# The first activation rows split straight from PSUM feature by feature, the first weight chunk split in two pieces, and the first transfers dealt out to two queues

## The chip, the cores and the metric

The kernel runs on one core of one Trainium2 chip. The metric is the device time of one execution in microseconds, as the median of several runs. TensorE (PE in the rows) does the matrix products, VectorE (DVE) and ScalarE (ACT) the element-wise work, GpSimd (POOL) a few small steps, and SyncE (SP) issues most of the transfers.

## What is computed

The reference is a decoder trunk of two layers on 256 rows of 1024 features in fp32. Each layer is

```
h = RMSNorm(x);  u = h @ w_in          # one wide input projection, columns for q, k, v, gates
o_A = sliding-window attention with sinks;  o_B = native sparse attention
x = x + RMSNorm((sigmoid(g_A) * (o_A @ W_A) + sigmoid(g_B) * (o_B @ W_B)) @ w_out)
x = x + RMSNorm(ConvGatedMLP(RMSNorm(x)))
```

The change touches only the first products of the first layer: the gain of the first RMSNorm is multiplied into `x`, the result is transposed so that features lie on the partitions, and it is multiplied with the first columns of `w_in`. The factor of the norm itself (one over the root mean square of a row) is applied later, to the products.

## The kernel before

Every fp32 operand is cut into a high and a low part (`copy` on ACT writes the high part as fp32r, `sub` on DVE writes the rest), and every product is made of three fp32r matmuls: high by high, high by low, low by high (`mm3`, L375; `products`, L438, for the first two chunks). Weights come in chunks through `Stream`: `load` (L154) issues the DMA on SP, `high` (L172) issues the ACT copy of a whole chunk and returns a function that issues the DVE subtraction. A chunk of `w_in` is 128 partitions by 2 feature blocks by 512 columns, 512 KB.

Rows are handled in two tiles `t` of 128, features in two halves `h` of four blocks of 128. The start is the function `start` (L1141). It issues some matmuls on zeros (`warm`, counts in `WARM`), transposes the gain vector to `gfirst`, and then for the first half of the features of both row tiles: `first_T` (L417) transposes four blocks of `X` into a PSUM bank of tag "T" (two buffers) and DVE multiplies the bank by the gain into an SBUF tile (L422); `first_split` (L425) copies that tile to the high part on ACT and returns the DVE subtraction for the low part. `W.high(0)` and `W.make(1)` split the first two weight chunks. The function `second` (run ahead of the first products of chunk 1) does the same for the second half of the features and for weight chunk 2. `W.make(3)` runs two steps later, and `rest` one step after that: the squares of `X` on ACT (`mean_sq`, L368), the root mean square on POOL (`rstd_of`, L362), and the rope tables (`rope_tables`, L336: a chain of DVE steps, two sines on ACT, eight multiplications on POOL).

The first tile of columns takes chunks 0 to 3 in the order of `FIRST`, row tile 0 and 1 in turn. When row tile 0 has its fourth chunk, `fin_a` (L562) makes the first rotated queries from the PSUM bank: `rope` (L486) on DVE reads the tables, ACT and DVE split the result, and `stack_T` (L497) transposes it on PE (L501). That transpose stands at a fixed place in PE's queue, between the products of the second tile of columns.

The order of the instructions in each engine's queue is not written out by hand (`MANUAL` is None). A planner sets it when the kernel is built, from the order of the text and its own idea of durations; the queue then stays as it is.

The transfers at the start: SP issues the identity and the gain, then the four chunks; ACT issues the four half-rows of `X` (L271), first half of both row tiles and then second half. A transfer takes one of eight completion semaphores in turn, so the ninth is issued when the first has landed.

Of the kernel before, what the change touches and what calls it, by code (L numbers as in the profile page):

```python
# [13 lines left out]
ALU = mybir.AluOpType  # L14
# [39 lines left out]
WARM = (6, 2, 3)  # L54
# [11 lines left out]
def tile_hybrid_trunk(  # L66
# [78 lines left out]
    class Stream:  # L145
# [26 lines left out]
        def high(self, i):  # L172
# [16 lines left out]
            copy(hi, st)  # L189

            def low():
                sub(lo, st, r32(hi))
                self.made[i] = (hi, lo, both)
                while self.front in self.made:
                    self.front += 1
# [73 lines left out]
    for h in range(2):  # L269
        for t in range(2):  # L270
            act.dma_start(halves(X[:, t, :])[h], halves(xv[:, t, :])[h])  # L271
    for i in range(4):
        W.load(i)
# [143 lines left out]
    def first_T(t, h):  # L417
        b = bank("T")
        for k in range(4):
            pe.transpose(b[:, k * P:(k + 1) * P], X[:, t, (h * 4 + k) * P:(h * 4 + k + 1) * P], ident)  # L420
        m = k2().rearrange("p (k c) -> p k c", k=4)
        dve.tensor_tensor(m, b.rearrange("p (k c) -> p k c", k=4), gfirst[:, h * 4:h * 4 + 4, None].to_broadcast([P, 4, P]), ALU.mult)  # L422
        return m

    def first_split(t, h, m, pair):  # L425
        tk = slice(t * P, (t + 1) * P)
        ho = pair[0][:, h * 4:h * 4 + 4, tk]
        copy(ho, m)
        return lambda: sub(pair[1][:, h * 4:h * 4 + 4, tk], m, r32(ho))

    def attn_layer(l, xp, rs, gains, first):
# [6 lines left out]
        def products(t, c, bk, chs, w):  # L438
            todo = [(tt, p, k) for p in ((0, 0), (0, 1), (1, 0)) for tt in range(2) for k in range(2)] if c == 0 else \
                   [(t, p, k) for p in ((0, 0), (1, 0), (0, 1)) for k in range(2)]  # L440
            if c == 0:
                todo = todo[6 * t:6 * t + 6]
            for tt, (xp_, wp_), k in todo:
# [697 lines left out]
    def start():  # L1141
# [12 lines left out]
        m0 = first_T(0, 0)  # L1154
        lw0 = W.high(0)
        low0 = first_split(0, 0, m0, xp)
        warm(WARM[1])
        low1 = first_split(1, 0, first_T(1, 0), xp)
        warm(WARM[2])
        lw0()  # L1160
        low0()
        low1()
        W.make(1)

        def second():
            m0, m1 = first_T(0, 1), first_T(1, 1)
            lw = W.high(2)
            lows = [first_split(t, 1, m, xp) for t, m in ((0, m0), (1, m1))]
            lw()
            for f in lows:  # L1170
                f()

# [96 lines left out]
```

## Time and profile before

| what | us |
|---|---|
| median of 3 runs | 783.96 (782.5 to 784.26) |
| the profiled execution, its own time | 782.81 |
| its span from the first to the last instruction | 781.0 |
| PE busy in the span | 759.2 |
| DVE busy | 613.1 |
| ACT busy | 495.4 |
| POOL busy | 34.0 |

The profiled execution is one of its own, 1.15 us below the median. Its time is 1.81 us more than its span. A busy engine in the table is one that has an instruction in flight. Matmuls overlap each other: a row of the timeline gives the start of the first of a group and the time to the end of the last, so the pace of the engine is read from starts, not from lengths. The same holds for ACT and DVE, where the next instruction starts some 0.1 us before the one before it ends.

### The profile page before, as it was taken

Reading aid. Unit: us, or ns where it says so; the run is one execution under the profiler, and the core shown is the slowest. Engines: PE = TensorE matmul, PEld = TensorE weight load, DVE = VectorE, ACT = ScalarE, POOL = GpSimd, SP = SyncE. Lnnn points to the kernel's source line nnn. Section 1 sums busy time; section 2 is a strip of 40 time slices with the busy share of each in tenths; the row PEclk is TensorE's granted clock in tenths of the full one; section 3 lists DMA queues with packets and bytes.
Section 4 is the critical chain, followed back from the end, with each engine's and each line's share of the span. In section 5 each row is a group of like instructions: output and inputs, shape, how many; then the busy total and the mean of one; then the engine's idle time right before and its main releaser. Section 6 shows DMA issues by size and latency. Waiting matters only on the chain.

```text
span 781.0 us, 12886 instructions
## 1 busy us (share of the span) xinstructions
PE 759.2 (97%) x4742; PEld 676.8 (87%) x4742; DVE 613.1 (79%) x1188; ACT 495.4 (63%) x950; POOL 34.0 (4%) x60
## 2 busy tenths in 40 slices
PE   8999999999899999999989999999999999999996
PEld 6788898887799999999868889988878999999995
DVE  6899898686787777777787989985876877677775
ACT  6596986754665555565556969866465655566552
POOL 4300001000100000000010000010010000000000
PEclk9999999999999999999999999999999999999999
DMA  8624264465566565665545323644645556656731
GB/s 337 196 86 133 64 219 170 136 188 162 173 205 189 188 187 184 209 210 188 164 134 163 95 82 121 200 153 162 200 144 172 188 187 189 188 182 201 217 104 54
DMA packets 42346, 131.26 MB, mean 168 GB/s; under 512 B 5375, under 2 KB 5931, under 8 KB 42283
## 3 DMA queue, kind: packets, MB, share of 16 engines
q1 hardware_dynamic: 41707, 129.39, 52.0%
q10 hardware_dynamic: 576, 1.05, 0.4%
q8 instruction: 37, 0.61, 0.3%
q14 instruction: 26, 0.21, 0.1%
HBM read 129.37 MB, written 1.05 MB: 167 GB/s over the span
## 4 chain that ended last, share of the span: by engine, by line
PE 83%; ACT 8%; DVE 4%; POOL 2%; issue 1%; DMA 1%; SPq 0%; DVEq 0%; POOLq 0%; ACTq 0%
PE mm L376 6%; PE mm L378 6%; PE mm L377 6%; PE T L1024 5%; PE mm L1023 5%; PE T L1023 5%; PE mm L1024 5%; PE T L1022 5%; PE mm L1022 5%; PE S L377 5%; PE S L376 5%; PE S L378 5%; PE O L376 3%; PE O L377 3%; PE O L378 3%; ACT k L635 2%
## 5 line engine op out<-in xcount | busy, mean ns | idle before, releaser
L117 DVE TENSOR_TENSOR wl<-st,wh 128x1024 fp32r<-128x1024 f32 (+2 forms) x220 | 260.4, 1186 | 101.5 <-ACT wh L114 100.3
L114 ACT ACTIVATE wh<-st 128x1024 fp32r<-128x1024 f32 (+2 forms) x220 | 225.5, 1028 | 178.1 <-PE O L378 40.5
L376 PE MATMUL mm<-wh,x 128*128 128x512 f32 (+2 forms) x248 | 92.9, 375 | 0.7 <-DVE VT L546 0.6
L377 PE MATMUL mm<-wl,x 128*128 128x512 f32 (+2 forms) x248 | 91.6, 370 | 0.0
L378 PE MATMUL mm<-wh,x 128*128 128x512 f32 (+2 forms) x248 | 91.3, 368 | 0.1
L1023 PE MATMUL mm<-q,wh 128*128 128x256 f32 x320 | 90.7, 284 | 0.0
L1024 PE MATMUL T<-q,wl 128*128 128x256 f32 x320 | 90.6, 283 | 0.0
L1023 PE MATMUL T<-q,wh 128*128 128x256 f32 x320 | 90.6, 283 | 0.0
L1024 PE MATMUL mm<-q,wl 128*128 128x256 f32 x320 | 90.6, 283 | 0.0
L1022 PE MATMUL T<-q,wh 128*128 128x256 f32 x320 | 90.5, 283 | 0.0
L1022 PE MATMUL mm<-q,wh 128*128 128x256 f32 x320 | 90.5, 283 | 0.0
L1022 PEld LDWEIGHTS mm<-q,wh 128*128 128x128 f32 x320 | 61.4, 192 | 0.9
L1022 PEld LDWEIGHTS T<-q,wh 128*128 128x128 f32 x320 | 61.4, 192 | 0.8
L1023 PEld LDWEIGHTS mm<-q,wh 128*128 128x128 f32 x320 | 61.4, 192 | 0.8
L1023 PEld LDWEIGHTS T<-q,wh 128*128 128x128 f32 x320 | 61.4, 192 | 0.7
L1024 PEld LDWEIGHTS mm<-q,wl 128*128 128x128 f32 x320 | 61.4, 192 | 0.1
L1024 PEld LDWEIGHTS T<-q,wl 128*128 128x128 f32 x320 | 61.4, 192 | 0.0
L378 PEld LDWEIGHTS mm<-wh,x 128*128 128x128 f32 x248 | 46.7, 188 | 6.1 <-DVE x L117 0.5
L376 PEld LDWEIGHTS mm<-wh,x 128*128 128x128 f32 x248 | 46.7, 188 | 6.0 <-issue 0.8
L377 PEld LDWEIGHTS mm<-wl,x 128*128 128x128 f32 x248 | 46.7, 188 | 4.8
L635 ACT ACTIVATE k<-k,mn 128x128 f32<-128x128 f32 (+1 forms) x96 | 42.4, 445 | 7.1 <-DVE mn L632 7.0
L114 ACT ACTIVATE k<-k 128x256 fp32r<-128x256 f32 x72 | 29.1, 413 | 9.1 <-DVE k L1035 5.6
(294 smaller groups left out, 1657.0 us busy)
## 6 DMA issues: line engine op xcount, KB each, us to landing
st<-in_ffn_w_up_dram SPq DMA_DIRECT2D x88, 512.0 KB, 4.2
st<-in_ffn_w_down_dram SPq DMA_DIRECT2D x44, 512.0 KB, 3.9
st<-in_w_in_dram SPq DMA_DIRECT2D x42, 512.0 KB, 3.6
st<-in_w_out_dram SPq DMA_DIRECT2D x16, 512.0 KB, 3.8
st<-in_w_in_dram SPq DMA_DIRECT2D x16, 384.0 KB, 3.1
st<-in_cmp_w_dram SPq DMA_DIRECT2D x16, 256.0 KB, 2.6
st<-in_w_branch_a_dram SPq DMA_DIRECT2D x8, 512.0 KB, 3.6
st<-in_w_branch_b_dram SPq DMA_DIRECT2D x8, 512.0 KB, 3.5
```

The source lines that it names most:

```text
L114: return act.activation(dst, src, AF.Copy, scale=scale)
L117: dve.tensor_tensor(dst, a, b, ALU.subtract)
L376: pe.matmul(o, xh, wh, start=first, stop=False, skip_group_check=True)
L377: pe.matmul(o, xh, wl, start=False, stop=False, skip_group_check=True)
L378: pe.matmul(o, xl, wh, start=False, stop=last, skip_group_check=True)
L635: last_exp[0] = act.activation(self.pt[:, hh, s, :], sm[:, :nk], AF.Exp, bias=self.mn[:, i:i + 1], scale=-1.0, accum_out=self.dn[:, i:i + 1])
L1022: pe.matmul(o, wh[:, k, :], hh[:, k, c0:c1], start=(k == 0), stop=False, skip_group_check=True)
L1023: pe.matmul(o, wh[:, k, :], hl[:, k, c0:c1], start=False, stop=False, skip_group_check=True)
L1024: pe.matmul(o, wl[:, k, :], hh[:, k, c0:c1], start=False, stop=(k == 7), skip_group_check=True)
```

## The change

`first_T` no longer multiplies by the gain: it returns the PSUM bank itself. `first_split` takes the bank and a list of feature blocks. For each block it issues one ACT copy from PSUM, 128 by 128, with the gain as the scale operand, which writes the high part; for the low part it returns a function that issues for each block one DVE `scalar_tensor_tensor` from PSUM (bank times gain minus high part). `W.high` takes a number of pieces; chunk 0 is split in two (one piece for each feature block of 128), the others in one as before. `start` orders the splits of the first half by block pairs, with the chunk copies in between, and leaves out the last three `warm` matmuls. `second` puts the splits of `X` ahead of the chunk's. `products` for chunk 0 takes the twelve matmuls in another order. The first half-row of `X` stays on ACT's queue; the other three go to SP's, between and behind the first two chunks.

```diff
-WARM = (6, 2, 3)
+WARM = (6, 2, 0)
...
-        def high(self, i):
+        def high(self, i, pieces=1):
...
-            copy(hi, st)
+            cuts = [slice(n * a // pieces, (n + 1) * a // pieces) for n in range(pieces)]
+            for c in cuts:
+                copy(hi[:, c], st[:, c])
 
             def low():
-                sub(lo, st, r32(hi))
+                for c in cuts:
+                    sub(lo[:, c], st[:, c], r32(hi[:, c]))
...
-    for h in range(2):
-        for t in range(2):
-            act.dma_start(halves(X[:, t, :])[h], halves(xv[:, t, :])[h])
-    for i in range(4):
-        W.load(i)
+    act.dma_start(halves(X[:, 0, :])[0], halves(xv[:, 0, :])[0])
+    W.load(0)
+    nc.sync.dma_start(halves(X[:, 1, :])[0], halves(xv[:, 1, :])[0])
+    W.load(1)
+    for t in range(2):
+        nc.sync.dma_start(halves(X[:, t, :])[1], halves(xv[:, t, :])[1])
+    W.load(2)
+    W.load(3)
...
-        m = k2().rearrange("p (k c) -> p k c", k=4)
-        dve.tensor_tensor(m, b.rearrange("p (k c) -> p k c", k=4), gfirst[:, h * 4:h * 4 + 4, None].to_broadcast([P, 4, P]), ALU.mult)
-        return m
-
-    def first_split(t, h, m, pair):
+        return b
+
+
+    def first_split(t, h, b, pair, ks):
         tk = slice(t * P, (t + 1) * P)
-        ho = pair[0][:, h * 4:h * 4 + 4, tk]
-        copy(ho, m)
-        return lambda: sub(pair[1][:, h * 4:h * 4 + 4, tk], m, r32(ho))
+        for k in ks:
+            act.activation(pair[0][:, 4 * h + k, tk], b[:, k * P:(k + 1) * P], AF.Copy, scale=gfirst[:, 4 * h + k:4 * h + k + 1])
+
+        def low():
+            for k in ks:
+                kk = 4 * h + k
+                dve.scalar_tensor_tensor(pair[1][:, kk, tk], b[:, k * P:(k + 1) * P], gfirst[:, kk:kk + 1], r32(pair[0][:, kk, tk]),
+                                         ALU.mult, ALU.subtract)
+        return low
...
-            todo = [(tt, p, k) for p in ((0, 0), (0, 1), (1, 0)) for tt in range(2) for k in range(2)] if c == 0 else \
-                   [(t, p, k) for p in ((0, 0), (1, 0), (0, 1)) for k in range(2)]
             if c == 0:
+                todo = [(tt, p, k) for p, tt in (((0, 0), 0), ((1, 0), 0), ((0, 0), 1), ((0, 1), 0), ((0, 1), 1), ((1, 0), 1)) for k in range(2)]
                 todo = todo[6 * t:6 * t + 6]
+            else:
+                todo = [(t, p, k) for p in ((0, 0), (1, 0), (0, 1)) for k in range(2)]
...
-        m0 = first_T(0, 0)
-        lw0 = W.high(0)
-        low0 = first_split(0, 0, m0, xp)
+        b0 = first_T(0, 0)
         warm(WARM[1])
-        low1 = first_split(1, 0, first_T(1, 0), xp)
+        b1 = first_T(1, 0)
         warm(WARM[2])
-        lw0()
-        low0()
-        low1()
-        W.make(1)
+        l00 = first_split(0, 0, b0, xp, (0, 1))
+        lw0 = W.high(0, 2)
+        l10 = first_split(1, 0, b1, xp, (0, 1))
+        l02 = first_split(0, 0, b0, xp, (2, 3))
+        l12 = first_split(1, 0, b1, xp, (2, 3))
+        lw1 = W.high(1)
+        for f in (l00, lw0, l10, l02, l12, lw1):
+            f()
 
         def second():
-            m0, m1 = first_T(0, 1), first_T(1, 1)
+            bs = [first_T(t, 1) for t in range(2)]
+            lows = [first_split(t, 1, bs[t], xp, range(4)) for t in range(2)]
             lw = W.high(2)
-            lows = [first_split(t, 1, m, xp) for t, m in ((0, m0), (1, m1))]
-            lw()
             for f in lows:
                 f()
+            lw()
```

## Rows read from the trace of the kernel before

**Rows 1.** The page: the span, the busy times of the engines, the clock granted to TensorE in 40 slices.

```profile
PE 759.2 (97%) x4742; PEld 676.8 (87%) x4742; DVE 613.1 (79%) x1188; ACT 495.4 (63%) x950; POOL 34.0 (4%) x60
...
PEclk9999999999999999999999999999999999999999
```

**Rows 2.** The chain of work that ended last, in order of time, from the start to the first transpose of rotated queries: start, length, what.

```profile
1.58 5.00 DMA st<-in_w_in_dram
...
6.60 1.06 ACT wh L114
...
12.53 1.23 ACT x L114 x2
13.76 0.52 ACT wh L114
...
20.84 3.36 POOL tab L359 x4
...
29.77 0.51 PE T L501 x4
```

**Rows 3.** The timeline of PE: start, length of the group, engine, line, operation, tiles, count, and in brackets the idle time ahead of it with what ended that.

```profile
1.44 2.92 PE L1148 MATMUL S<-k 128*128 128x512 f32 x6 [1.44 <-DVE k L1143]
4.55 0.24 PE L1152 MATMUL T<-cst,k 8*128 8x8 f32 x1 [0.19 <-DMA k<-in_attn_pre_gain_dram]
4.73 1.11 PE L420 MATMUL T<-cst,X 128*128 128x128 f32 x4
...
6.28 0.60 PE L420 MATMUL T<-cst,X 128*128 128x128 f32 x4
6.63 0.94 PE L1148 MATMUL S<-k 128*128 128x512 f32 x3
8.23 1.26 PE L445 MATMUL mm<-wh,x 128*128 128x512 f32 x4 [0.66 <-ACT x L114]
...
11.17 1.03 PE L420 MATMUL T<-cst,X 128*128 128x128 f32 x8
...
14.81 0.39 PE L376 MATMUL mm<-wh,x 128*128 128x512 f32 x1
15.04 0.39 PE L377 MATMUL mm<-wl,x 128*128 128x512 f32 x1
...
28.41 0.39 PE L376 MATMUL S<-wh,x 128*128 128x512 f32 x1
29.77 0.51 PE L501 MATMUL T<-ident_r,k 128*128 128x128 f32 x4 [0.98 <-DVE k L117]
```

**Rows 4.** The timeline of ACT, same columns.

```profile
6.60 1.06 ACT L114 ACTIVATE wh<-st 128x1024 fp32r<-128x1024 f32 x1 [2.49 <-DMA st<-in_w_in_dram]
7.56 1.13 ACT L114 ACTIVATE x<-k 128x512 fp32r<-128x512 f32 x2
...
10.40 1.06 ACT L114 ACTIVATE wh<-st 128x1024 fp32r<-128x1024 f32 x1 [0.52 <-DMA st<-in_w_in_dram]
12.53 1.23 ACT L114 ACTIVATE x<-k 128x512 fp32r<-128x512 f32 x2 [1.07 <-DVE k L422]
13.66 1.05 ACT L114 ACTIVATE wh<-st 128x1024 fp32r<-128x1024 f32 x1
14.62 0.61 ACT L372 ACTIVATE k<-X 128x512 f32<-128x512 f32 x1
...
17.07 2.94 ACT L114 ACTIVATE wh<-early 128x1024 fp32r<-128x1024 f32 x3
```

**Rows 5.** The stretches of the start: busy time of each engine (number of instructions), the clock granted to PE, the DMA share, and in the last column GB/s moved.

```profile
2.00:3.00 1.00, 1.00 (x4) 0.78 (x3) 0.00 (x0) 0.39 (x1) 1.00 (x2) 1.00 0.40 119
3.00:4.00 1.00, 1.00 (x4) 0.54 (x2) 0.00 (x0) 0.99 (x2) 1.00 (x2) 1.00 0.99 359
4.00:5.00 1.00, 0.81 (x4) 0.45 (x4) 0.58 (x2) 0.11 (x1) 1.00 (x3) 1.00 1.07 426
```

**Rows 6.** The timeline of DVE, same columns.

```profile
5.88 0.69 DVE L422 TENSOR_TENSOR k<-T,gfirst 128x512 f32<-128x512 f32 x1 [0.88 <-PE T L420]
...
17.64 0.74 DVE L349 SCALAR_TENSOR_TENSOR k<-k 128x64 f32<-128x64 f32 x3
18.30 1.22 DVE L117 TENSOR_TENSOR wl<-early,wh 128x1024 fp32r<-128x1024 f32 x1
19.43 0.19 DVE L350 TENSOR_SCALAR k<-k 128x64 f32<-128x64 f32 x1
```

**Rows 7.** Instructions of the kinds that the change adds, where they stand elsewhere in this kernel: one row of the ACT timeline with 24 columns from PSUM and a scale operand, the one behind it with 256, and the next; then the group on the first V tile (128 columns from PSUM with a scale operand: lengths min/median/max in ns) and the DVE group with the same shape (busy us, mean ns).

```profile
59.41 0.27 ACT L114 ACTIVATE ns<-mm,rstd 128x24 f32<-128x24 f32 x1
59.57 0.47 ACT L114 ACTIVATE SG<-mm,rstd 128x256 f32<-128x256 f32 x1
59.93 0.23 ACT L595 ACTIVATE ge<-ns 128x24 f32<-128x24 f32 x1
...
L114 ACT ACTIVATE VT<-S,rstd x4: 348/364/370, 36.7 to 425.7; 128x128 fp32r<-128x128 f32 x4
...
L492 DVE SCALAR_TENSOR_TENSOR k<-mm,rstd,tab 128x128 f32<-128x128 f32 x16 | 4.8, 343 | 0.0
```

**Rows 8.** The timeline of POOL, same columns.

```profile
16.03 0.72 POOL L364 TENSOR_SCALAR rstd<-s 128x1 f32<-128x1 f32 x1 [10.67 <-ACT k L372]
...
20.81 3.39 POOL L359 TENSOR_SCALAR tab<-k 128x64 f32<-128x64 f32 x4
```

## The prediction

> **What bounds the kernel now.** I read the page first. PE is busy for 759.2 of 781.0 us and is granted its full clock (2.4 GHz) in every slice, so after the start the time is PE's, and a change at the start is worth what it brings PE forward by, provided that nothing takes the lead away again [rows 1]. The reader should look for the last place where PE still waits for something that began at the start. The chain of waits names it: first weight chunk landed, its ACT copy, ACT splits of `X`, a further chunk copy, the rope tables on POOL, and only at 29.77 PE's transpose of the first rotated queries [rows 2]. PE's own timeline says the same from the other side: its last matmul ahead of that transpose starts at 28.41, and then it stands still for 0.98 us, waiting for DVE [rows 3]. So a lead of PE alone ends in that wait. What counts is when the tables are done, and they hang on the squares of `X`, which ACT begins at 14.62 behind all splits of the first four chunks [rows 4].
>
> **First part: the transfers.** Bytes do not change. The first chunk lands at 1.58 + 5.00 = 6.58 [rows 2], having shared the DMA engines with four half-rows. After the change only 64 + 4 + 256 + 512 KB = 0.86 MB lie ahead of its end. By the rates of the stretches 0.48 MB have moved by 4.0 and 0.90 MB by 5.0, so its last byte moves at 4.9 [rows 5]. The bytes of the identity and the first half-row (0.33 MB) would by the same rates have moved by 3.6, and the transposes that need them start at 4.73, or 4.55 for the gain [rows 3]: up to 1 us from last byte to use. That puts the chunk at 5.5 to 5.9, some 0.9 earlier, without a wait beyond the 5.88 that comes next. The second half-row, now behind the chunk, moves 0.26 MB at 0.4 MB/us, 0.65 later (6.2 to 6.6), about where its transposes stand today, 6.28. Chunk 2 lands where it did, near 10.4, since the same bytes are ahead of it [rows 4]. The issues moved from ACT to SP cost three times some 0.4 us of a queue whose bytes wait for the DMA engines anyway; I cost them at nothing. If a hole of 0.3 us opens in the stream while the first chunk starts, it would delay chunk 2 by as much.
>
> The Trainium skill, "Trainium Kernel Development and Optimization", section Key Constraints, says that transfers from the SP and ACT queues run on the same 16 DMA engines and interleave, and that a second issuing queue only saves issue time. By it the two queues gain nothing; what can gain is that the half-rows stand behind the chunk in one queue. The shared time of the first chunk agrees [rows 2, 5].
>
> **Second part: the splits.** Before, a bank is ready when DVE can start at 5.88, is multiplied there, and ACT copies the result, after the first chunk [rows 4, 6]. After, ACT starts on the bank at 5.88. A copy of 512 columns takes ACT 0.51 from start to start (the pair of 1.13 less one length of 0.62), one of 1024 columns 0.95 ((2.94 - 1.05) / 2) [rows 4]. A copy from PSUM with a scale operand goes from start to start in 0.16 with 24 columns and 0.36 with 256; the line between them gives 0.25 with 128, and one alone is 0.36 long [rows 7]. The bounds for one are 0.16 and 0.36; I take 0.25. So 16 small copies are 4.0 us where four copies of 512 are 2.0: **ACT gets 2.0 us more work**, in return for a start 0.7 earlier and for waits it now has (0.52 and 1.07 us) [rows 4].
>
> ACT step by step, starts: block pair 5.88 and 6.13; chunk 0 in two pieces 6.38 and 6.89 (ends 7.00 and 7.51); row tile 1's pair 7.40, 7.65; the other pairs 7.90 to 8.65; chunk 1 at 8.90, free at 9.85. PE: first product at 7.04 instead of 8.23, the second at 7.55, then high by low and row tile 1 behind row tile 1's copies (8.01), and twelve products end their issue at about 10.05, at 0.227 each (0.23 between the starts at 14.81 and 15.04) [rows 3]. Before, the transposes that follow start at 11.17 at the latest: **1.1 us of lead**. Their banks free on DVE: eight `scalar_tensor_tensor` of 0.34, start to start 0.26, are 2.1 us, where the multiplications and subtractions of 512 columns were four times 0.6 = 2.4; DVE is no later [rows 6, 7].
>
> From there the lead shrinks. First bank of the second half: 10.05 + 0.7 = 10.75. ACT idles from 9.85 to 10.75, then eight copies to 12.76, chunk 2 (now behind them in the text) to 13.82, chunk 3 from 13.71, and the squares start at **14.65, against 14.62** [rows 4]. DVE can make the low part of chunk 2 only after 13.82, plus 1.22 = 15.04. PE, through chunk 1 at 13.9, does one product of chunk 2 and then waits for that low part: its second product of chunk 2 starts at **15.05, against 15.04** [rows 3]. Of 1.1 us nothing is left. With the small copies at 0.16 the squares would come 0.6 earlier (only the second eight lie on the path, the wait at 9.85 absorbs the others), at 0.36 some 1.6 later (both groups then count). If the planner puts chunk 2's copy into ACT's hole, at its landing of 10.4, the squares start at 14.3, 0.35 earlier, and PE doesn't wait.
>
> The Trainium skill, "ScalarE: Activation LUTs", section What ACT_TABLE_LOAD costs, gives for an ACTIVATE 186 ns + 0.833 ns per column, 93 ns more for a scale operand, and an overlap of 93 ns. By it a small copy would be 0.29 from start to start, an estimate, and the squares would come 0.3 to 0.6 later. The row of 256 columns agrees within 0.04 us with what it gives (0.40 against 0.36) [rows 7].
>
> **Third part: the rest.** The three warm matmuls left out (0.94 us) lie in PE's wait for the first split [rows 3]; I cost them at nothing, as PE's idle time ahead of its first product shrinks from 0.66 to about nothing. Cover gone, PE could run at the pace of its first six matmuls, 2.92 / 6 = 0.49, which would be 12 x 0.26 = 3.1 us; the granted clock shows no such stretch [rows 1]. The order of products moves nothing in sum. From the squares on, POOL's steps follow at once (16.03) and the tables (20.81, 3.39 for four) set DVE's rope [rows 2, 8]. So the first rotated queries come at 29.8 within some tenths, and after that the kernel is as before.
>
> **The sum.** Squares 0.0 (from -0.6 to +1.6, with the planner's choice -0.35), hence PE's transpose at 29.77 + 0.0. With a little weight on the hole being used: -0.15 us on the profiled execution, 782.81 - 0.15 = 782.66. That execution is 1.15 below the median of the runs; the same difference from the median gives **783.8**.
>
> **The rivals.**
> *The whole lead arrives (faster).* If the planner fills ACT's hole with chunk 2 and with squares, whose half-rows land before chunk 2, the tables come forward by 1 us or more, PE's wait of 0.98 goes, and with it all 1.1 us of the products: -2.1, 783.96 - 2.1 = 781.9. For it: DVE's queue shows that the planner does move work forward (a chunk's subtraction stands between two steps of the rope tables that are neighbours in the text) [rows 6]. Against it: ACT waited 1.07 us at 11.46 with `X` there, and the squares were not moved up [rows 4].
> *ACT becomes the bound (slower).* Place: the second eight small copies. At 0.36 each they and the first eight bring the squares to 16.2 and the tables with them: +1.6 and, with PE's transpose fixed in its queue, all of it is paid, 783.96 + 1.6 = 785.6. It decides from 0.25 upward, where the hole at 9.85 closes (8 x 0.11 = 0.9 more). The same size comes if the planner puts a chunk's DVE step of 1.22 once more ahead of the rope steps. For it: 0.36 is the length of the very shape [rows 7]. Against it: all neighbours on ACT overlap by 0.1.
> *The change doesn't do what it says.* The planner may keep chunk 0 whole ahead of the small copies, or the half-row behind the chunk is late; then the products start at 7.5 to 8.2, and the end is the same, 784.0.
>
> **How the numbers follow.** Forecast 0.60, whole lead 0.20, ACT bound 0.14, no effect 0.06. A measurement of this kernel can tell about 0.2% (1.6 us) from no change. The forecast and the last rival lie within that, but for 0.02 on either side that I leave to reordering further down; the first rival is faster in 0.18 of its 0.20, the second slower in 0.12 of its 0.14. That gives faster 0.20, same 0.66, slower 0.14. The range goes from the whole lead (781.7, a little below 781.9) to +1.4 (785.3), short of the slow rival's end; it leaves out less than 2 in 10.
>
> **What would show it.** ACT's first small copy at about 5.9 and the first product at 7.0; the transposes of the second half at 10.1; start to start of the small copies 0.25; squares at 14.3 to 14.7; PE's second product of chunk 2 near 15.0 and its wait ahead of the first transpose of rotated queries still about 1 us. The prediction is wrong if the squares start before 13.5 or after 16, if the rope steps on DVE stand in another order, or if PE's gaps after 30 us differ.

## The result, and the profile after

The changed kernel takes 789.55 us in the median of ten runs (785.6 to 790.67), the kernel before 783.92 in ten beside it: a ratio of 1.0069, 95% interval 1.0051 to 1.0087. The change makes the kernel slower by 0.7%, 5.6 us. The forecast was no change, 783.8, with a range up to 785.3; the result lies outside it on the slow side.

The profiled execution of the changed kernel took 790.49 us with a span of 788.7, which is 7.7 more than before and 0.9 above its own median. On the page, two lines answer to [rows 1]:

```profile
PE 764.1 (97%) x4739; PEld 679.7 (86%) x4739; DVE 612.7 (78%) x1197; ACT 498.0 (63%) x963; POOL 32.8 (4%) x60
...
PEclk8999999999999999999989999999999999999999
```

PE is busy 4.9 us longer than before with the same products, and its granted clock is no longer full in all slices: the first slice shows it, and one in the middle. So this is not only waiting; part of the work itself ran slower. The timeline of PE shows where (columns as in [rows 3]; L426 transposes `X`, L457 are the products of the first two chunks):

```profile
1.44 2.92 PE L1160 MATMUL S<-k 128*128 128x512 f32 x6 [1.44 <-DVE k L1155]
...
4.50 0.80 PE L426 MATMUL T<-cst,X 128*128 128x128 f32 x4
5.05 0.71 PE L1160 MATMUL S<-k 128*128 128x512 f32 x2
8.15 1.01 PE L426 MATMUL T<-cst,X 128*128 128x128 f32 x4 [2.39 <-DMA X<-in_x_dram]
8.82 1.20 PE L457 MATMUL mm<-wh,x 128*128 128x512 f32 x2
10.79 2.08 PE L457 MATMUL mm<-wh,x 128*128 128x512 f32 x4 [0.77 <-DVE x L438]
12.66 1.91 PE L457 MATMUL mm<-wl,x 128*128 128x512 f32 x4
14.37 0.95 PE L457 MATMUL mm<-wh,x 128*128 128x512 f32 x2
15.16 1.03 PE L426 MATMUL T<-cst,X 128*128 128x128 f32 x8
...
20.31 0.50 PE L383 MATMUL mm<-wl,x 128*128 128x512 f32 x1 [0.85 <-DVE wl L117]
...
34.38 0.53 PE L513 MATMUL T<-ident_r,k 128*128 128x128 f32 x4 [0.17 <-DVE k L117]
```

The reader is to see four things. PE stands still for 2.39 us ahead of row tile 1's transposes, and what ends the wait is a transfer: the second half-row. Then two products, and a wait for DVE's first low part. Then the products start (12.66 - 10.79) / 4 = 0.47 apart, where the forecast had 0.227. And the transpose of the first rotated queries stands at 34.38 against 29.77 [rows 3], so 4.6 us of the loss are there by then. The wait of 0.98 that stood ahead of it is nearly gone (0.17): PE is now as late as the tables. These are late by the same amount, as the chain of waits has it (the row answers to 20.84 in [rows 2]):

```profile
25.37 3.52 POOL tab L365 x4
```

ACT's timeline answers to [rows 4]:

```profile
5.33 0.63 ACT L433 ACTIVATE x<-T,gfirst 128x128 fp32r<-128x128 f32 x2 [2.68 <-PE T L426]
5.85 1.15 ACT L114 ACTIVATE wh<-st 128x512 fp32r<-128x512 f32 x2
9.20 1.67 ACT L433 ACTIVATE x<-T,gfirst 128x128 fp32r<-128x128 f32 x6 [2.21 <-PE T L426]
...
15.79 2.18 ACT L433 ACTIVATE x<-T,gfirst 128x128 fp32r<-128x128 f32 x8 [3.98 <-PE T L426]
17.81 2.05 ACT L114 ACTIVATE wh<-st 128x1024 fp32r<-128x1024 f32 x2
19.70 0.67 ACT L378 ACTIVATE k<-X 128x512 f32<-128x512 f32 x1
```

The first small copies and the chunk's two pieces come even earlier than forecast. Then ACT stands idle twice, 2.21 and 3.98 us, both times for PE's transposes, and the squares begin at 19.70 instead of 14.62. The eight small copies start at 15.79 and the next instruction at 17.81, so (17.81 - 15.79) / 8 = 0.25 from start to start: the value chosen in the prediction was right. DVE answers to [rows 6]:

```profile
10.38 0.61 DVE L438 SCALAR_TENSOR_TENSOR x<-T,gfirst,x 128x128 fp32r<-128x128 f32 x2 [5.61 <-ACT x L433]
10.91 1.28 DVE L117 TENSOR_TENSOR wl<-st,wh 128x512 fp32r<-128x512 f32 x2
...
16.97 2.16 DVE L438 SCALAR_TENSOR_TENSOR x<-T,gfirst,x 128x128 fp32r<-128x128 f32 x8 [2.09 <-ACT x L433]
```

The first low part needs only the bank, which was ready at 5.33, and the high part that ACT had made by 5.96. It starts at 10.38. What it waited for is the last of ACT's copies out of the same bank, and this one stands in ACT's queue behind row tile 1's first copies, which wait for the half-row. The second eight show the same: DVE starts at 16.97, behind the fourth copy, the last one from its bank, and not behind the eighth.

The issues on SP of the half-row and of the chunk behind it, and then the last line of the view on the tile `X`: the time from issue to last landing, shortest, middle and longest. The view has it for two of the three transfers of `X` on SP's queue, so its middle is their mean:

```profile
1.98 0.43 SPq L274 DMA_DIRECT2D X<-in_x_dram  x1
2.44 0.43 SPq L159 DMA_DIRECT2D st<-in_w_in_dram  x1
```

```profile
DMA to landing us min/median/max: 6.0/6.6/7.2
```

The half-row is the shortest: it is issued at 1.98 and has landed 6.0 later, at 8.0. Last, the stretches (columns as in [rows 5]): the first ten us, then single ones, there and at the boundary of the two layers.

```profile
0.00:10.00 10.00, 6.17 (x19) 4.00 (x19) 1.07 (x3) 3.95 (x10) 4.84 (x10) 0.91 0.76 254
...
5.00:6.00 1.00, 0.76 (x5) 0.33 (x3) 0.00 (x0) 0.67 (x3) 0.36 (x1) 1.00 0.68 186
6.00:7.00 1.00, 0.00 (x0) 0.00 (x0) 0.00 (x0) 0.99 (x2) 0.00 (x0) 1.00 0.93 303
7.00:8.00 1.00, 0.00 (x0) 0.00 (x0) 0.00 (x0) 0.00 (x0) 0.00 (x0) 1.00 0.93 340
...
9.00:10.00 1.00, 1.00 (x3) 0.29 (x2) 0.00 (x0) 0.80 (x4) 0.00 (x0) 0.50 1.05 426
14.00:15.00 1.00, 1.00 (x4) 0.81 (x3) 0.88 (x1) 0.00 (x0) 0.00 (x0) 0.50 1.01 401
15.00:16.00 1.00, 1.00 (x10) 0.86 (x9) 0.00 (x0) 0.21 (x1) 0.00 (x0) 0.96 1.02 410
...
398.00:399.00 1.00, 0.73 (x4) 0.73 (x5) 1.00 (x3) 0.56 (x2) 0.66 (x3) 0.50 0.00 0
403.00:404.00 1.00, 1.00 (x4) 0.78 (x3) 0.51 (x1) 0.55 (x2) 0.30 (x1) 0.50 0.00 0
```

From 5 to 7 the transfers run at 186 and 303 GB/s, where the kernel before has 383 and 379. In the stretch from 7 to 8 no engine works; only transfers run. After this standstill the granted clock is 0.50, the lower level of 1.2 GHz, in every single us from 9 to 15, and that is where the products start 0.47 apart. The same level shows once more from 398 to 404, behind two gaps of PE of 1.58 and 1.28 us that end at 396.33 and 398.27 and belong to the norm of the second layer. There 12 products start 0.43 apart instead of 0.23, which is 2.4 us. The gaps are of the same size in the kernel before (1.58 and 1.27, ending at 391.68 and 393.60), and its clock stays full behind them. So the account of the profiled execution is: 4.61 us late at the first rotated queries, 4.65 on arrival at the boundary, 7.7 at the end. The times of the ten runs go loosely with the mean granted clock: the shortest, 785.6, had 0.998, the two of 790.67 had 0.990, but one of 790.39 had 0.995.

### The profile page after: what moved, and what is told of

It reads as the page before. It is cut to its first block, busy times and chain, and to the rows that moved or that the text cites. A ratio compares the mean times of both kernels' runs of the same rounds, so it can differ in the third digit from the quotient of the medians.

```text
span 788.7 us, 12901 instructions
## 1 busy us (share of the span) xinstructions
PE 764.1 (97%) x4739; PEld 679.7 (86%) x4739; DVE 612.7 (78%) x1197; ACT 498.0 (63%) x963; POOL 32.8 (4%) x60
## 4 chain that ended last, share of the span: by engine, by line
PE 82%; ACT 7%; DVE 4%; DMA 3%; POOL 1%; issue 1%; DVEq 0%; POOLq 0%; SPq 0%; ACTq 0%
PE mm L382 7%; PE mm L383 6%; PE mm L384 6%; PE T L1036 5%; PE T L1035 5%; PE mm L1036 5%; PE mm L1035 5%; PE T L1034 5%; PE mm L1034 5%; PE S L383 5%; PE S L382 5%; PE S L384 5%; PE O L382 3%; PE O L383 3%; PE O L384 3%; ACT k L647 2%
## 5 line engine op out<-in xcount | busy, mean ns | idle before, releaser
L117 DVE TENSOR_TENSOR wl<-st,wh 128x1024 fp32r<-128x1024 f32 (+3 forms) x221 | 260.4, 1181 | 103.2 <-ACT wh L114 101.8
L114 ACT ACTIVATE wh<-st 128x1024 fp32r<-128x1024 f32 (+3 forms) x221 | 225.7, 1025 | 176.4 <-PE O L384 38.8
```

Of the source, the lines that this page charges most:

```text
L114: return act.activation(dst, src, AF.Copy, scale=scale)
L117: dve.tensor_tensor(dst, a, b, ALU.subtract)
```

## The experiments

Theory one says that the transfers did it: the half-row behind the first chunk comes too late, PE stands still, everything else follows. Theory two says that the new splits did it: ACT's small copies, DVE's wait for them and the order of `second`. A third question is what the granted clock adds. All runs were timed in five rounds beside the kernel before; ratios are to that kernel, with 95% intervals. The changed kernel has 1.0069 (1.0051 to 1.0087). In e1, e3, e6, e11 and e12 the traces have every engine's instructions in the changed kernel's order (in e6 but for the twelve more on PE); where the planner orders some anew, it is said.

### The transfers

**e1_transfers_back**: the changed kernel with the transfers of the kernel before.

```diff
-    act.dma_start(halves(X[:, 0, :])[0], halves(xv[:, 0, :])[0])
-    W.load(0)
-    nc.sync.dma_start(halves(X[:, 1, :])[0], halves(xv[:, 1, :])[0])
...
+    for h in range(2):
+        for t in range(2):
+            act.dma_start(halves(X[:, t, :])[h], halves(xv[:, t, :])[h])
+    for i in range(4):
+        W.load(i)
```

> The changed kernel with the transfers issued as before (four half-rows on ACT's queue, four chunks on SP's). Every queue of the other engines stays in the same order as in the changed kernel. Theory A (the second half-row stands behind the first chunk, lands 1.8 us late, and PE stands still for 2.4 us and runs at half pace after it): the transposes of the second half-row start near 6.0, no product waits for them, median 783 to 785. Theory B (the split from PSUM: DVE's low parts wait for all copies of the bank, and ACT has 2.0 us more to do): DVE's first low part still starts only behind the fourth copy, squares at 16 or later, median 787 to 790. Theory C (the three warm matmuls left out, the slow pace by itself): products still 0.45 apart, median 786 to 789.

785.8 us, ratio 1.0021 (1.0009 to 1.0033). Most of the loss is gone, though the median is above theory A's 783 to 785. What theory B had expected stands beside it: DVE's first low part starts at 8.53, behind the fourth copy, and the squares at 16.20.

**e2_transfers_alone**: the kernel before with the transfers of the changed one.

```diff
-    for h in range(2):
-        for t in range(2):
-            act.dma_start(halves(X[:, t, :])[h], halves(xv[:, t, :])[h])
...
+    act.dma_start(halves(X[:, 0, :])[0], halves(xv[:, 0, :])[0])
+    W.load(0)
+    nc.sync.dma_start(halves(X[:, 1, :])[0], halves(xv[:, 1, :])[0])
...
```

> The kernel before with the transfers of the change and nothing else changed in its text; the planner may order some instructions up to 60 us otherwise. Theory A: the half-row behind the first chunk lands near 8, PE stands still for 2 us ahead of its transposes and then runs at half pace, median 787 to 789. Theory B: the transfers cost nothing by themselves, median 783.5 to 785.

787.54 us, ratio 1.0049 (1.0032 to 1.0066). The planner orders some later steps anew here, and PE's products start 0.43 apart up to 13.90, so the size is not clean, but PE's timeline has the wait in the same place:

```profile
8.32 1.09 PE L423 MATMUL T<-cst,X 128*128 128x128 f32 x4 [1.85 <-DMA X<-in_x_dram]
```

**e3_half_row_on_act**: the changed kernel with one transfer moved, row tile 1's first half-row, to ACT's queue behind row tile 0's.

```diff
+    act.dma_start(halves(X[:, 1, :])[0], halves(xv[:, 1, :])[0])
     W.load(0)
-    nc.sync.dma_start(halves(X[:, 1, :])[0], halves(xv[:, 1, :])[0])
```

> The changed kernel with one transfer moved: the second half-row is issued on ACT's queue behind the first, no longer on SP's behind the first chunk; the two late half-rows stay on SP's queue. Theory A: the half-row lands by 5.5, its transposes start near 6.0, median 783 to 785, like e1. Theory B: median 787 to 790, DVE's first low part near 8.5. If all three moved half-rows matter and not this one alone, the median lies between, 785 to 787, with the second half's transposes late.

785.35 us, ratio 1.0018 (1.0008 to 1.0027), no different from e1. So one half-row carries the whole loss by the transfers; the two second half-rows on SP and their issues there cost nothing that can be seen. Its PE timeline and its first stretch:

```profile
6.26 0.72 PE L426 MATMUL T<-cst,X 128*128 128x128 f32 x4
...
8.78 1.22 PE L457 MATMUL mm<-wh,x 128*128 128x512 f32 x4 [0.92 <-DVE x L438]
...
30.72 0.54 PE L513 MATMUL T<-ident_r,k 128*128 128x128 f32 x4 [0.17 <-DVE k L117]
```

```profile
0.00:10.00 10.00, 7.62 (x24) 5.18 (x24) 3.22 (x7) 5.65 (x13) 4.84 (x10) 1.00 0.80 295
```

The transposes no longer wait, the clock reads 1.00, and 295 GB/s move in the first 10 us, against 254: the late half-row was not only late itself, the whole stream behind it had a hole of 0.4 MB.

**e11_half_row_ahead**: the half-row on SP's queue, but ahead of the chunk.

```diff
+    nc.sync.dma_start(halves(X[:, 1, :])[0], halves(xv[:, 1, :])[0])
     W.load(0)
-    nc.sync.dma_start(halves(X[:, 1, :])[0], halves(xv[:, 1, :])[0])
```

> The change as it is, but row tile 1's first half-row is issued on SP's queue ahead of the first weight chunk instead of behind it. Theory A, the half-row is late because its bytes stand behind the chunk's in one queue: it lands by 5.0, PE does not stand still ahead of its transposes, squares near 16.0, ratio to before about 1.002, as with the half-row on ACT's queue (1.0018). Theory B, it is late because SP's queue serves some of its transfers late whatever their order: the half-row, or the chunk in its place, lands some 2 us after the first parts of it, PE stands still for over 1 us once more, ratio 1.004 to 1.007.

786.05 us, ratio 1.0034 (1.0022 to 1.0046). PE's row has no wait for a transfer any more; ACT's shows that now the chunk comes late:

```profile
6.26 1.06 PE L426 MATMUL T<-cst,X 128*128 128x128 f32 x4
```

```profile
6.77 1.15 ACT L114 ACTIVATE wh<-st 128x512 fp32r<-128x512 f32 x2 [0.50 <-DMA st<-in_w_in_dram]
```

Theory A of its expectation holds for the half-row: its order in the queue made it late, not the queue. The squares begin at 16.68, 0.6 later than in e3, by the later chunk; the ratio lies between the two.

**e12_both_behind_on_act**: chunk 0 and the half-row behind it both on ACT's queue.

```diff
-            nc.sync.dma_start(st, src)
+            (act if i == 0 else nc.sync).dma_start(st, src)
...
-    nc.sync.dma_start(halves(X[:, 1, :])[0], halves(xv[:, 1, :])[0])
+    act.dma_start(halves(X[:, 1, :])[0], halves(xv[:, 1, :])[0])
```

> The change as it is, but the first weight chunk and, behind it, row tile 1's first half-row are issued on ACT's queue, behind row tile 0's first half-row; SP has chunk 1, the second half-rows and chunks 2 and 3. Theory A, a transfer behind a 512 KB chunk in its queue is late whichever queue it is: PE stands still for 1 us or more ahead of row tile 1's transposes, ratio 1.004 to 1.007. Theory B, the lateness belongs to SP's queue: the half-row lands near 6.4, PE stands still for less than 1 us, ratio 1.001 to 1.003.

789.38 us, ratio 1.0072 (1.0056 to 1.0088); PE waits 1.58 us for the half-row. That is theory A's number, but the run doesn't tell the theories apart as I had meant it: SP's queue sends chunk 1 meanwhile, and its 512 KB share the engines with the half-row, which the 6.4 of theory B left out.

How the half-row was late is in the landings. The trace keeps, for each transfer, when each of its 16 parts landed; here the first, the eighth and the last:

| kernel | transfer | queue, place | issued | first | eighth | last |
|---|---|---|---|---|---|---|
| before | half-row | ACT, behind a half-row | 1.16 | 4.31 | 4.58 | 5.20 |
| e3 | half-row | ACT, behind a half-row | 1.16 | 4.21 | 4.44 | 4.56 |
| e11 | half-row | SP, ahead of chunk 0 | 1.57 | 4.10 | 4.36 | 4.64 |
| after | half-row | SP, behind chunk 0 | 1.98 | 5.59 | 6.55 | 8.01 |
| e2 | half-row | SP, behind chunk 0 | 1.96 | 5.79 | 6.46 | 8.19 |
| e4 | half-row | SP, behind chunk 0 | 1.98 | 5.51 | 6.19 | 8.53 |
| e6 | half-row | SP, behind chunk 0 | 1.98 | 6.00 | 6.78 | 8.01 |
| e12 | half-row | ACT, behind chunk 0 | 1.64 | 7.01 | 7.72 | 8.18 |
| after | chunk 0 | SP, first | 1.58 | 4.68 | 5.03 | 5.70 |
| e3 | chunk 1 | SP, behind chunk 0 | 1.96 | 6.88 | 7.12 | 7.64 |

In all four kernels that have the half-row behind chunk 0 on SP's queue, its eighth part lands between 6.19 and 6.78. That is where the forecast by bytes and rate had its last part (6.2 to 6.6), but not for the forecast's reason: in the changed kernel chunk 0's eighth part had landed at 5.03, so the half-row's came 1.5 behind it and not 0.65. From 4.50 to 6.50 the transfers of these four kernels moved 171 to 284 GB/s (213 in the changed kernel), those of the nine others 358 to 413. The last part comes 1.2 to 2.3 us after the eighth, and a reader of the tile waits for the last. The half-rows of the table that stand behind no chunk have landed 0.35 to 0.9 after their first part. A wide spread is not tied to a chunk ahead in the queue, though: the third half-row on ACT's queue of the kernel before landed from 6.43 to 8.26 while SP's queue sent its chunks.

### The splits

**e4_low_at_once**: the changed kernel with each function for a low part called right behind its own copies, so that in the text no copy from the same bank stands between.

```diff
         l00 = first_split(0, 0, b0, xp, (0, 1))
+        l00()
         lw0 = W.high(0, 2)
+        lw0()
...
-        for f in (l00, lw0, l10, l02, l12, lw1):
-            f()
+        lw1()
```

> The changed kernel with each low part of the first half written behind its own copies in the text, so that DVE reads a bank before ACT's later copies of it; the transfers stay as changed. Theory A: PE still waits 2.4 us for the second half-row, the wait of 0.8 us for DVE goes, median 787.5 to 789.5. Theory B: DVE's first low part starts near 6.3 instead of 10.4, median 784 to 786. The planner may order some instructions up to 60 us otherwise than in the changed kernel.

787.68 us, ratio 1.0049 (1.0036 to 1.0063), an interval that overlaps that of the changed kernel. In its trace DVE's first low part starts at 6.04 instead of 10.38, so the reading of that wait is right; PE's wait for the half-row is still there, 2.85 us. The planner orders many steps anew here, on PE from 32 us on, so the time is no clean measure of the repair.

**e10_low_at_once_half_row**: e3 and e4 together.

```diff
+    act.dma_start(halves(X[:, 1, :])[0], halves(xv[:, 1, :])[0])
     W.load(0)
-    nc.sync.dma_start(halves(X[:, 1, :])[0], halves(xv[:, 1, :])[0])
...
+        l00()
...
-        for f in (l00, lw0, l10, l02, l12, lw1):
-            f()
```

> The changed kernel with the second half-row on ACT's queue (as e3) and each low part of the first half written behind its own copies (as e4). What e3 still loses to the kernel before (0.18%, 1.4 us) is, by theory B, the wait of DVE's first low part for the later copies of its bank: it goes, DVE starts at about 6.3 instead of 8.4, PE's wait of 0.9 us goes, the squares start at 15.0 to 15.3 instead of 16.0, median 784.0 to 784.8. The rival: it is ACT's additional work (16 small copies) and the place of chunk 2's copy, and then nothing comes of it: squares at 16 again, median 785.4.

783.99 us, ratio 1.0009 (0.9998 to 1.002). Here the start runs as the prediction had worked it out; PE first, then ACT:

```profile
6.83 1.95 PE L457 MATMUL mm<-wh,x 128*128 128x512 f32 x6 [0.47 <-ACT wh L114]
...
9.99 1.03 PE L426 MATMUL T<-cst,X 128*128 128x128 f32 x8
...
29.48 0.54 PE L513 MATMUL T<-ident_r,k 128*128 128x128 f32 x4 [0.39 <-DVE k L117]
```

```profile
10.63 2.17 ACT L433 ACTIVATE x<-T,gfirst 128x128 fp32r<-128x128 f32 x8 [0.39 <-PE T L426]
12.64 2.06 ACT L114 ACTIVATE wh<-st 128x1024 fp32r<-128x1024 f32 x2
14.53 0.68 ACT L378 ACTIVATE k<-X 128x512 f32<-128x512 f32 x1
```

First product 6.83 (forecast 7.04), transposes 9.99 (10.05), second eight small copies 10.63 (10.75), squares 14.53 (14.65). The order by bank holds the other way, too: ACT's last two copies of the first half, from a bank that DVE is reading, wait 0.33 for DVE. The planner has put one chunk step of DVE (18.12) between two rope steps that are neighbours in the kernel before, and that is all that it orders anew.

**e8_both_repairs**: e10, and in `second` chunk 2's copy and low part ahead of the second eight small copies and their low parts.

```diff
         def second():
             bs = [first_T(t, 1) for t in range(2)]
-            lows = [first_split(t, 1, bs[t], xp, range(4)) for t in range(2)]
             lw = W.high(2)
+            lows = [first_split(t, 1, bs[t], xp, range(4)) for t in range(2)]
+            lw()
             for f in lows:
                 f()
-            lw()
```

> As e10, and in addition chunk 2's copy and subtraction stand ahead of the splits of the second half, as in the kernel before. If ACT's wait for the transposes (2.3 us in e3) is the hole that the copy can fill, the squares start at 14.2 to 14.6, PE doesn't wait for the low part of chunk 2 (0.84 us in e3), and its first transpose of rotated queries starts at 29.3 to 29.9: median 783.0 to 784.0, the kernel before or a little under. If the small copies themselves are the bound, the squares stay at 15 or later and the median is 784.5 to 785.5.

782.86 us beside 782.87, ratio 0.9994 (0.9984 to 1.0004). Its interval lies wholly below that of e3, so the two repairs of the splits together are shown, about 0.24%, with what little the planner orders anew (six products up to 35 us stand elsewhere); how they share it is only read from the traces. ACT and PE:

```profile
10.50 1.06 ACT L114 ACTIVATE wh<-st 128x1024 fp32r<-128x1024 f32 x1 [0.25 <-DMA st<-in_w_in_dram]
11.46 2.15 ACT L433 ACTIVATE x<-T,gfirst 128x128 fp32r<-128x128 f32 x8
...
14.41 0.68 ACT L378 ACTIVATE k<-X 128x512 f32<-128x512 f32 x1
```

```profile
29.08 0.54 PE L513 MATMUL T<-ident_r,k 128*128 128x128 f32 x4 [1.00 <-DVE k L117]
```

Chunk 2's copy fills ACT's hole at its landing, PE's wait for that chunk's low part (0.85 in the changed kernel) is gone, and the transpose comes 0.7 ahead of before, with a wait of 1.00 as before. The 0.7 doesn't show in the median: in the profiled execution the granted clock fell to 0.50 at the layer boundary (0.68 in the mean from 390 to 395). It does show between runs of the same mean clock. At 0.996 the eight runs of e8 took 782.84 to 783.82, the seven of the kernel before 783.65 to 784.46; but only 3 of e8's 11 runs had 0.997 or more, against 17 of 29. The runs were put into these groups after the fact, and why fewer of e8's had the higher clock isn't shown.

**e13_squares_early**: e8 with the squares of the first half-rows in ACT's hole, the rival of the whole lead as a kernel.

```diff
+        def squares(n):
+            j = k4()
+            for t in range(2):
+                last_sq[0] = act.activation(j[:, t * 512:(t + 1) * 512], halves(X[:, t, :])[n], AF.Square, scale=1.0 / 32.0,
+                                            accum_out=s2s[t][:, n:n + 1])
...
             bs = [first_T(t, 1) for t in range(2)]
+            squares(0)
...
+            squares(1)
             for t in range(2):
-                rs[t] = rstd_of(mean_sq(halves(X[:, t, :])))
+                rs[t] = rstd_of(s2s[t])
```

> The kernel with all three repairs (half-row on ACT's queue, low parts behind their own copies, chunk 2's copy ahead of the second eight small copies), and the squares of the first half-rows moved into ACT's idle time near 10 us, as the rival of the whole lead has it. The planner orders some steps after 15 us anew, DVE's among them, so this is a try for a faster kernel and no clean test of one edit. If the tables set the end of the start, they come 0.5 to 1.0 earlier and PE's wait of 1.00 ahead of the first rotated queries shrinks by as much: ratio to before 0.998 to 0.999. If the new order costs more than that: 1.000 to 1.005.

788.03 us, ratio 1.0053 (1.0039 to 1.0067). The squares are done 0.3 earlier than in e8 (16.67 against 17.00), and the first rotated queries come 2.2 later (31.28 against 29.08). DVE's timeline says why:

```profile
17.64 1.23 DVE L117 TENSOR_TENSOR wl<-early,wh 128x1024 fp32r<-128x1024 f32 x1
18.79 0.19 DVE L349 TENSOR_SCALAR k<-k 128x64 f32<-128x64 f32 x1
18.89 1.22 DVE L117 TENSOR_TENSOR wl<-early,wh 128x1024 fp32r<-128x1024 f32 x1
20.02 0.19 DVE L350 TENSOR_SCALAR k<-k 128x64 f32<-128x64 f32 x1
```

The planner now puts chunk steps of 1.22 between the rope steps of 0.2, so that the step that stood at 16.94 in e8 (L350) begins at 20.02. That delay would be 2.2 of the 5.2 us by which e13's median lies above e8's. Its granted clock fell as well, to 0.57 in the mean from 50 to 58 and once more at the layer boundary, and all six runs have a mean clock of 0.991 to 0.993; how the rest divides isn't shown. No version with a median clearly below the kernel before was found.

### The granted clock

**e6_warm**: the changed kernel with 14 matmuls on zeros instead of 2 in PE's wait for the half-row.

```diff
-WARM = (6, 2, 0)
+WARM = (6, 14, 0)
```

> The changed kernel with 14 warm matmuls instead of 2 ahead of the transposes of the second half-row, so that PE has work until these can start; nothing else differs. Theory C (the pace is what costs): the first twelve products stand 0.23 apart instead of 0.45, the transposes of the second half of the features start near 12.5 instead of 15.2, median 786 to 787.5. Theory A: the late half-row costs what it costs, PE's products still start behind 8.1, the pace is worth under 1 us, median 788.5 to 789.5.

786.12 us, ratio 1.0036 (1.0025 to 1.0048): about half of the loss is given back (0.33 of 0.69% by the ratios, 3.4 of 5.6 us by the medians), with the half-row as late as ever (8.01). The products stand 0.23 apart, as theory C had it; the transposes of the second half start at 13.91, not near 12.5. The stretches, and PE's first rotated queries:

```profile
0.00:10.00 10.00, 8.56 (x31) 6.40 (x31) 1.56 (x3) 3.56 (x8) 4.84 (x10) 1.00 0.75 249
10.00:20.00 10.00, 7.98 (x36) 5.78 (x36) 8.76 (x21) 7.66 (x21) 0.06 (x1) 1.00 1.04 400
...
400.00:405.00 5.00, 5.00 (x28) 4.20 (x27) 3.53 (x6) 2.27 (x6) 1.10 (x3) 1.00 0.33 120
```

```profile
33.14 0.54 PE L513 MATMUL T<-ident_r,k 128*128 128x128 f32 x4 [0.17 <-DVE k L117]
```

The clock reads 1.00 throughout; the first rotated queries are 3.4 later than before, and the span is 3.3 longer: in this kernel the loss at the start is the whole loss. The changed kernel loses 1.2 more at the start (34.38 - 33.14), although its transposes start earlier (8.15 against 8.96, where the last zeros still run), and the rest at the boundary.

**e9_warm_alone**: the kernel before without its last three warm matmuls.

```diff
-WARM = (6, 2, 3)
+WARM = (6, 2, 0)
```

> The kernel before without the three warm matmuls, nothing else. If they only fill PE's wait (the prediction's cost of nothing): median within 0.8 us of the kernel before, the first twelve products 0.23 apart. If they hold the pace: the products stand 0.45 apart and the median is 785 to 787.

784.11 us, ratio 1.0014 (1.0004 to 1.0025). The first four products take 1.61 instead of 1.26 [rows 3], but the first rotated queries come only 0.1 later (29.86 against 29.77). The span is 1.2 longer all the same; in this execution the clock was 0.82 and 0.84 from 390 to 400. That the two belong together is argued, not shown. Neither expectation was met: the pace isn't half, and the median is more than 0.8 above that of the kernel before.

The runs say more, since each has its mean granted clock on record. The 29 runs of the kernel before that were timed beside e2, e8, e9 and e10 took 782.3 to 783.4 us at a mean clock of 0.997 or 0.998 (17 runs), 783.7 to 784.5 at 0.996 (7 runs) and 784.9 to 785.4 below (5 runs). So the clock falls in some executions of the kernel before, too, and its profiled execution (0.998) is one in which it didn't. At 0.996, six runs of e9 took 783.9 to 784.7, much as those; e9 has only 2 of 11 runs at 0.998. The three matmuls are worth little at a given clock here, and what e9 loses goes with how often the clock falls.

## Why the prediction was wrong

**The step that failed** is in the part on the transfers: the second half-row "moves 0.26 MB at 0.4 MB/us, 0.65 later (6.2 to 6.6), about where its transposes stand today, 6.28". It landed at 8.01, 2.3 behind chunk 0 (5.70) instead of 0.65. Two things were missing. The rate was taken from other stretches, and did not hold: 213 GB/s moved from 4.50 to 6.50 in the changed kernel, and the half-row's eighth part came 1.5 behind the chunk's (6.55 against 5.03). That this eighth part lies inside 6.2 to 6.6 is luck, as most of the chunk's parts had landed earlier than forecast. And what counts is the last of the 16 parts, whose lag of 1.5 behind the eighth had no term in the sum, though the step had no slack: it was set against 6.28 with nothing to spare. The text named lateness of this half-row as a rival, but with products at 7.5 to 8.2 and "the end is the same", weight 0.06; both the lateness and what follows from it were too small. e3, which moves this one transfer, takes the ratio from 1.0069 to 1.0018: about 4.2 of the 5.6 us. e11 does the same by order within SP's queue alone, and its ratio is 1.0034.

**The rest of the transfers held.** Chunk 0 was forecast for 5.5 to 5.9 and landed at 5.70. The issues on SP cost nothing (e1 and e3 agree). Chunk 2, forecast near 10.4, came at 12.06 in the changed kernel, but at 10.30 in e3: the hole that begins with the half-row moved it, since e3 has the same two half-rows ahead of it on SP's queue. Of the Trainium skill's rule in "Trainium Kernel Development and Optimization", section Key Constraints, that the queues share 16 DMA engines and interleave, e12 agrees: there the half-row's first part came at 7.01, while the other queue's chunk moved. What the rule leaves open is the order within one queue, and this cost 3.4 us of landing (8.01 against 4.64 in e11).

**"DVE is no later" failed** as well. Its first low part was forecast by the lengths of the steps; it waits for the last ACT copy out of the same bank. What this costs in the changed kernel isn't shown (e4's ratio is lower, 1.0049, but its interval overlaps and its order differs); in e3 it costs PE 0.92 at 8.78, and the squares begin at 16.04 instead of 14.53 in e10.

**The half pace was priced and set aside**, and came another way. The prediction had it under the removed warm matmuls: "12 x 0.26 = 3.1 us", set aside since the clock showed no such stretch and since PE's idle time would shrink. The 0.49 under that price is the length of a group divided by its count; by their starts (2.03 to 3.73 for the second to the sixth) these matmuls stood 0.43 apart, which makes it 2.4. And the clock row couldn't show the stretch, as told in the last section. In the changed kernel PE's idle time grew to 2.39, and eight products from 10.79 to 14.37 at 0.45 apart instead of 0.23 are 1.8 us. The three removed matmuls would not have filled that wait: they stood behind row tile 1's transposes [rows 3], and the wait is ahead of them, where e6 put its twelve. No run puts the three back into the changed kernel. e6 shows that the clock is worth 3.4 of the 5.6 us in the medians (789.55 - 786.12); in the profiled executions, 1.2 of it is lost by the first rotated queries and some 3 at the layer boundary, which the prediction had not in view. These 3.4 and e3's 4.2 overlap: in e3's profiled execution the clock doesn't fall, either.

**What held.** The small copies (0.25 from start to start, as chosen; the Trainium skill's "ScalarE: Activation LUTs", What ACT_TABLE_LOAD costs, had led to an estimate of 0.29). The reading that a lead at the start ends in the wait for the tables: with the half-row on ACT's queue and the low parts at once, e10 follows the forecast's times within 0.21 us up to the squares, and e8 its variant with chunk 2 in the hole (squares 14.41, forecast 14.3; no wait for the low part); their ratios, 1.0009 and 0.9994, are the "no change" that was forecast. So the price of ACT's extra 2.0 us and the loss of the lead on the way were right: with the half-row on ACT's queue and the wait for the bank gone, the forecast's time is met. Of the rivals, the slow one was right in its sign and wrong in its place: ACT was not the bound, it stood idle for 2.21 and 3.98 us.

**What stays open.** Why the last parts of a half-row behind a chunk lag by up to 2.3 us, in three or four of the 16 parts, while a chunk behind a chunk (e3, 0.5) and a chunk behind a half-row (e11, 0.55) lag less, isn't settled, and e12 was to help and doesn't: there the half-row behind chunk 0 on ACT's queue has its last part only 0.46 behind the eighth. The single packets don't settle it, either. In the changed kernel some 17 of the half-row's 128 packets of 2 KB took 0.4 to 1.2 us, where most such packets take 0.08, but in e4, which has the longest lag, no packet of 2 KB took more than 0.32 from 2.5 to 8. Nor is it settled why the same gaps of PE at the layer boundary lower the clock in the profiled executions of the changed kernel, e4, e8, e9, e10, e12 and e13, and not in those of the kernel before, e1, e2, e3, e6 and e11. As the runs of the kernel before differ among themselves in the same way, one execution of each can't tell what the kernel adds. Over the runs the kernels do differ: eight of e6's nine had a mean clock of 0.998, one of the changed kernel's ten, and 9 of the 26 of the kernel before that were timed beside e6 had 0.997 or 0.998.

## What to carry to other kernels

A transfer that is moved behind a large one in a queue has to be given the landing of its last part, not of its bytes at a rate from another stretch; where its reader has no slack, leave it where nothing large is ahead of it. The price of PE at half pace belongs in the range together with the lateness that would bring it, wherever PE may have to wait for a transfer; matmuls on zeros give it back only where they stand in that wait. When a whole tile's split is cut by features, write each low part behind its own copies: a reader of a PSUM bank waited here for every copy from that bank that stood earlier in the text.

## What was not expected of the hardware

A half-row of 256 KB behind a chunk of 512 KB in one queue landed over 2.4 us (5.59 to 8.01; in e4 over 3.0), and the lag stayed in that queue: the parts of chunk 3, five transfers later, landed in the changed kernel from 11.44 to 13.40. After PE had stood still for 2.39 us the granted clock was 0.50 for some 7 us, and after 2.85 us in e4 for less (0.50 from 9 to 11, 1.00 from 12).

A granted clock of 1.00 at the start of a trace can mean that there is no record of it. In e2 products started 0.43 apart ((12.19 - 10.48) / 4, from its PE timeline) while the views read 1.00 from 10 to 15; but the first record of the clock in e2's trace begins at 14.14, and a view gives 1.00 for time without one. There the pace changes: up to 13.90 the starts are 0.43 apart, from 14.25 on 0.23. In the kernel before the first record begins at 5.98, and the first six matmuls on zeros, 0.43 apart in every kernel here, lie ahead of it. So [rows 1, 5] say nothing of the clock ahead of 5.98, and there the pace is to be read from the starts. And 400 us behind the change, at gaps that are the same in both kernels, the granted clock was 0.50 in one profiled execution and 1.00 in the other.
